# Two reorderings on the matrix engine: earlier transposes in the two output projections, later transposes in the first modulation

## The chip, the cores and the metric

The kernel runs on one core of a Trainium2 chip. The metric is the device time of one execution in microseconds (us), lower is better. A core has a matrix engine (PE in the profile, with PEld for its weight loads), a vector engine (DVE), a scalar engine (ACT), a small general engine (POOL) and a queue engine (SP). Each runs its own list of instructions in order, and they meet through semaphores. Matrix results land in PSUM, everything else lives in SBUF.

## The reference

Two layers of a diffusion backbone over 512 latent and 256 context tokens (six tiles of 128 tokens), model width 1024, everything in float32. Cut to what matters here:

```python
m_lat = split(silu(c)     @ mod_w[l] + mod_b[l], 6)     # shift, scale, gate for mixer and FFN
m_ctx = split(silu(c_ctx) @ mod_w[l] + mod_b[l], 6)
h = modulate(rms(x, norm_pre_mix[l]), m[0], m[1])
o = mixer(h)            # layer 0: gated linear attention (GLA) + softmax attention; layer 1: HGRN2
x = x + m[2] * rms(o @ w_out, norm_post_mix[l])         # output projection, post-norm, gate
h = modulate(rms(x, norm_pre_ffn[l]), m[3], m[4])
x = x + m[5] * rms((silu(h @ w_gate) * (h @ w_up)) @ w_down, norm_post_ffn[l])
```

Layer 0 carries all six tiles, layer 1 ends with the four latent tiles.

## The kernel before

A float32 product is done as three matrix instructions on operands that are split into a high and a low part (`wH`, `wL` for weights: a cast on ACT, then a subtraction on DVE).

**The order.** A scheduler (the tile framework) places instructions on the engines from the order in which the program issues them and from its own costs. Where `self.pinned` is set, the matrix engine keeps the program's order; the other engines are still arranged by the scheduler. In the even mixer of layer 0 the program's order is a string of step names, each of which advances a generator by one step:

```python
run("qk0 qk0 e m qk0 e e v0 ... m m kv q m m q m q m m m m m m m m m qk1 kv m")
```

Here `q` is a block of 48 matrix instructions of the attention's query projection (`nat<-wH,x`, 128x256 each; its first call only loads weights), `kv` the same for keys and values, `qk1` the second half of the GLA queries and keys, and `m` one step of `mod_vec`.

**The early modulation (`mod_vec`).** It makes m[2] and m[3] of layer 0. For each of the two jobs DVE adds up eight scaled rows of `mod_w` into two accumulators (`macc<-mraw`, L535/L537, one `m` step a row block). Then one `m` step sums them over partitions on PE (`mod_acc`, 8 matrix instructions) and DVE copies the sum out (`modrows`, L469). The next step turns it on PE (`modT`, four transposes), and DVE adds the bias (`modcol`, L481) and multiplies the norm's gain in (`gc`, L644). The step after that turns this too (`gcT`, one transpose), DVE copies it (`gt`, L650) and ACT issues its write to DRAM (`gd<-gt`, L652); the same step then starts the second job. `modrows`, `gt` and, later, the attention's table tile `rope` share one ring of two buffers (tag `mraw`). `mod_acc`, `modT` and `gcT` share a ring of two PSUM buffers (tag `tr`).

**The output projections (`out_proj`, called by `project` once a layer).** Tiles are taken in pairs, six tiles in the order 4, 5, 0, 1, 2, 3 in layer 0, and 0, 1, 2, 3 in layer 1. A tile's product is two halves of 24 matrix instructions (`oproj`, 128x512). The first pair's is cut so that the late weight units come last; the other pairs run tile by tile, half by half. After a tile, `end` runs its post-norm, residual and pre-norm: ACT squares (`junk<-oproj`), DVE multiplies (`pn`), POOL takes the power (`rs`), DVE adds (`xr`), ACT squares again (`xn<-xr`), POOL again, DVE writes the normalized tile (`xn<-xr,rs`, L695). It leaves a *turn* in the list `self.turns`: eight transposes on PE in two PSUM buffers (`hT<-ident,xn`), eight activations on ACT (`f<-hT`, L707), and a split (`b<-f`, L97 on ACT and L98 on DVE) into the operands of the feed-forward block. `turn(left)` runs turns from the front of that list until `left` are left:

```python
def turn(self, left=0):
    while len(self.turns) > left:
        self.turns.pop(0)()
```

The third tile of a layer's projection (and the fifth in layer 0) is the point at which two turns, of the two tiles before it, are waiting. The last pair's turns run in the feed-forward block's first products (`pearly`).

Of the kernel before, what the change touches and what calls it, by code (L numbers as in the profile page):

```python
# [316 lines left out]
class Net:  # L317
# [761 lines left out]
    def even_mixer(self, h, mix, z):  # L1079
# [132 lines left out]
        def run(steps):  # L1212
            for x in steps.split():
                if x not in running:
                    running[x] = kinds[x]()
                next(running[x], None)

        self.pinned = True
        run("qk0 qk0 e m qk0 e e v0 qk0 e e m qk0 e e m v0 e e m m q v0 m m v0 m m kv q m m q m q m m m m m m m m m qk1 kv m")
        tp.release()  # L1220
        gp = self.open_pool("gla")
        run("c0 l0 kv m c0 kv c0 v1 qk1 c0 p p qk1 c0 l0 p qk1 l0 c0 g0 qk1 l0 p c1 p v1 l0 p v1 l0 c1 p v1 l0 c1 l1 g1 g0 c1 g0 r0 c1 l1 r0 g0 l1")
# [335 lines left out]
    def out_proj(self, wop, pp, w, cat, tiles, end, mods=iter(())):  # L1558
        self.tc.keep_in_program_order(self.nc.scalar.preload_act_table_set("silu_and_others"))
        units = [self.rows_unit(w, c) if c < 4 else self.rows_unit(w, c, wop) for c in range(KD)]  # L1560
        for t0 in range(0, len(tiles), 2):
            pair = tiles[t0 : t0 + 2]
            pts = [self.mm_tile("oproj") for _ in pair]
            for cs in ((0, 1, 2, 3), (4, 5, 6, 7)) if t0 == 0 else (range(KD),):
                for t, pt in zip(pair, pts):
                    tok = slice(t * P, (t + 1) * P)
                    for hf in range(2):
                        n = slice(hf * 512, hf * 512 + 512)
                        for c in cs:
                            self.mm3(  # L1570
                                pt[:, n],
                                cat.hl(c, tok),
                                (units[c][0][:, 0, n], units[c][1][:, 0, n]),
                                c == 0,
                                c == KD - 1,
                            )
                        if hf or t0:
                            next(mods, None)
                    if cs[0] == 0 and t == pair[len(cs) == 4]:
                        self.turn()  # L1580
            for t, pt in zip(pair, pts):
                for _ in end(pt, t):
                    pass
# [622 lines left out]
```

## Time and profile before

| | |
|---|---|
| median of 3 runs | 1681.66 us (1681.48 to 1682.79) |
| the profiled execution's own time | 1680.08 us |
| its span | 1678.3 us |
| PE busy | 1638.8 us, 98% |
| DVE busy | 1312.2 us, 78% |
| ACT busy | 916.9 us, 55% |
| granted PE clock | 0.999 |
| early modulation's turns | 102 to 118 us |
| layer 0's projection | 340 to 417 us |
| layer 1's projection | 1285 to 1334 us |

The profile is one execution; all times in it count from the start of its span. "Busy" is time in which an engine has an instruction under way. In a timeline, each row is a start, a length, an engine, a line, an operation with output and inputs, and a count; in brackets stands how long the engine was idle before it and what it waited for. Matrix instructions overlap, so the distance between starts is their price, not their length.

### The profile page before, as it was taken

How to read it: one execution, taken by the hardware profiler on the slowest of the kernel's cores; microseconds unless marked ns; L12 is line 12 of the kernel's file. 1: busy time of each engine (PE TensorE's matmuls, PEld its weight loads, DVE VectorE, ACT ScalarE, POOL GpSimd, SP SyncE). 2: the span in 40 equal slices, each digit the busy share in tenths (PEclk: the TensorE clock that was granted, in tenths of full speed). 3: DMA queues.
4: the chain of work that ended last, by engine and by line, in shares of the span. 5: the costliest groups of instructions: out<-in, count | busy, mean ns of one | idle time of the engine just before them, and what ended most of it. 6: DMA issues, size and time to landing. Idle time of an engine off the chain costs nothing.

```text
span 1678.3 us, 32400 instructions
## 1 busy us (share of the span) xinstructions
PE 1638.8 (98%) x13347; PEld 1474.3 (88%) x13347; DVE 1312.2 (78%) x2104; ACT 916.9 (55%) x1560; POOL 122.6 (7%) x129
## 2 busy tenths in 40 slices
PE   6999998999999999999999999999999999999998
PEld 5889987888999999998887788888888899999886
DVE  4889768966898989778668648788775499987887
ACT  4745557846544443445447536566564565555564
POOL 1004210001000000002101000000000100000310
PEclk9999999999999999999999999999999999999999
DMA  9651002154253446249516542111115334433973
GB/s 331 193 155 41 2 28 101 52 198 152 90 151 101 134 148 193 78 136 222 101 56 210 193 132 64 52 54 50 52 56 159 117 113 122 115 101 101 223 166 138
DMA packets 184736, 204.77 MB, mean 122 GB/s; under 512 B 7143, under 2 KB 141837, under 8 KB 184589
## 3 DMA queue, kind: packets, MB, share of 16 engines
q1 hardware_dynamic: 173632, 181.82, 34.6%
q0 software_dynamic: 9024, 17.30, 5.9%
q10 hardware_dynamic: 1932, 3.59, 0.6%
q8 instruction: 104, 1.70, 0.4%
q14 instruction: 44, 0.35, 0.1%
HBM read 193.23 MB, written 9.46 MB: 121 GB/s over the span
## 4 chain that ended last, share of the span: by engine, by line
PE 84%; DVE 7%; ACT 4%; DMA 2%; issue 2%; POOL 1%; DVEq 0%; ACTq 0%; POOLq 0%
PE nat L355 12%; PE a L355 11%; PE ff L355 8%; PE E L355 8%; PE x L355 6%; PE oproj L355 6%; PE o L355 4%; PE b L355 4%; PE D L355 4%; PE pearly L355 3%; PE fq L355 3%; PE gqk L355 2%; PE q L355 2%; PE S L355 2%; PE poh L355 1%
## 5 line engine op out<-in xcount | busy, mean ns | idle before, releaser
L355 PE MATMUL nat<-wH,x 128*128 128x256 f32 (+2 forms) x968 | 226.1, 322 | 3.1 <-ACT x L734 2.6
L355 PEld LDWEIGHTS nat<-wH,x 128*128 128x128 f32 x968 | 162.0, 190 | 20.5 <-ACT x L734 4.2
L824 ACT CAST wH<-raw 128x1024 fp32r<-128x1024 f32 x120 | 124.9, 1051 | 99.0 <-DVE raw L849 37.6
L825 DVE TENSOR_TENSOR wL<-raw,wH 128x1024 fp32r<-128x1024 f32 x120 | 145.7, 1221 | 23.2 <-ACT wH L824 22.6
L355 PE MATMUL nat<-wL,x 128*128 128x256 f32 (+2 forms) x484 | 153.5, 317 | 1.8 <-DVE wL L770 1.8
L770 DVE TENSOR_TENSOR wL<-raw,wH 128x1024 fp32r<-128x1024 f32 (+1 forms) x83 | 98.7, 1198 | 49.7 <-ACT wH L769 49.0
L355 PE MATMUL ff<-x,wH 128*128 128x512 f32 (+1 forms) x512 | 127.7, 340 | 0.0
L769 ACT CAST wH<-raw 128x1024 fp32r<-128x1024 f32 (+1 forms) x83 | 84.9, 1035 | 70.6 <-PE ff L355 19.9
L668 POOL TENSOR_TENSOR rs<-ms,neghalf 128x1 f32<-128x1 f32 (+2 forms) x62 | 64.7, 1049 | 791.1 <-DVE ms L666 791.0
L355 PE MATMUL oproj<-wH,x 128*128 128x512 f32 x320 | 102.3, 396 | 0.6 <-ACT x L1290 0.6
L355 PEld LDWEIGHTS nat<-wL,x 128*128 128x128 f32 x484 | 92.1, 190 | 7.9 <-DVE wL L770 2.7
L355 PEld LDWEIGHTS ff<-x,wH 128*128 128x128 f32 x512 | 87.2, 190 | 10.0
L597 DVE SCALAR_TENSOR_TENSOR macc<-mraw,scT,macc 128x1024 f32<-128x1024 f32 x70 | 88.0, 1280 | 8.8 <-DMA mraw<-in_mod_w_dram 8.4
L355 PE MATMUL x<-wH,two 128*128 128x512 f32 x280 | 90.6, 392 | 0.8 <-DVE y L1801 0.7
L976 ACT COPY qkh<-arr 128x512 f32<-128x512 f32 x112 | 70.1, 642 | 36.4 <-DVE arr L981 32.2
L1723 POOL DMA_DIRECT2D t<-in_ffn_w_down_dram x36 | 41.8, 1198 | 637.2 <-DVE t L1762 337.5
L355 PE MATMUL ff<-x,wL 128*128 128x256 f32 (+1 forms) x256 | 86.2, 337 | 0.0
L849 DVE TENSOR_TENSOR raw<-raw 128x512 f32<-128x512 f32 x120 | 82.8, 690 | 2.8
L981 DVE TENSOR_TENSOR arr<-arr,f 128x512 f32<-128x512 f32 x112 | 74.2, 687 | 1.9 <-ACT qkh L976 0.3
L355 PEld LDWEIGHTS oproj<-wH,x 128*128 128x128 f32 x320 | 59.5, 188 | 12.8 <-ACT x L1290 1.1
L355 PE MATMUL E<-x,wH 128*128 128x384 f32 (+1 forms) x320 | 70.7, 310 | 0.0
L355 PE MATMUL b<-x,wH 128*128 128x384 f32 (+1 forms) x320 | 70.6, 310 | 0.0
(420 smaller groups left out, 4530.2 us busy)
## 6 DMA issues: line engine op xcount, KB each, us to landing
mraw<-in_mod_w_dram SPq DMA_DIRECT2D x80, 512.0 KB, 4.1
raw<-in_ffn_w_gate_dram SPq DMA_DIRECT2D x44, 512.0 KB, 4.8
raw<-in_ffn_w_up_dram SPq DMA_DIRECT2D x44, 512.0 KB, 4.4
raw<-in_odd_w_in_dram SPq DMA_DIRECT2D x40, 512.0 KB, 3.7
t<-in_ffn_w_down_dram POOLq DMA_DIRECT2D x30, 512.0 KB, 8.7
raw<-in_ffn_w_down_dram SPq DMA_DIRECT2D x28, 512.0 KB, 7.9
mraw<-in_mod_w_dram SPq DMA_DIRECT2D x32, 256.0 KB, 6.3
raw<-in_even_w_in_dram SPq DMA_DIRECT2D x16, 512.0 KB, 6.8
```

Of the source, the lines that this page charges most:

```text
L355: return self.pin(self.nc.tensor.matmul(*a, **k))
L597: nc.vector.scalar_tensor_tensor(a, u, w, a, op0=ALU.mult, op1=ALU.add)
L668: nc.gpsimd.tensor_tensor(rs, ms, self.neghalf.to_broadcast([P, w]), op=ALU.pow)
L769: nc.scalar.copy(H[:, :m], raw[:, :m])
L770: nc.vector.tensor_tensor(L[:, :m], raw[:, :m], H[:, :m].bitcast(F32), op=ALU.subtract)
L824: self.nc.scalar.copy(H, f)
L825: self.nc.vector.tensor_tensor(L, f, H.bitcast(F32), op=ALU.subtract)
L849: add = lambda o, x, y: nc.vector.tensor_tensor(o, x, y, op=ALU.add)
L976: nc.scalar.copy(qkv[:, :, :, half, :], dst)
L981: nc.vector.tensor_tensor(dst, dst, tb, op=ALU.mult)
L1723: add = lambda o, src: self.pin(nc.gpsimd.dma_start(out=o, in_=src, accum_op=ALU.add))
```

## The change

Two edits, no instruction added or removed.

```diff
@@ even_mixer
-        run("... m m kv q m m q m q m m m m m m m m m qk1 kv m")
+        run("... m m kv q m q m q m m m m m m m m m m qk1 kv m")
@@ out_proj, after each half (hf) of each tile
+                        if not hf and t0 and t == pair[0]:
+                            self.turn(1)
                         if hf or t0:
                             next(mods, None)
                     if cs[0] == 0 and t == pair[len(cs) == 4]:
                         self.turn()
```

The first edit puts each of the two steps after `mod_acc` one `q` block later: `modT` behind a block, and `gcT` behind the next, right ahead of the second job's `mod_acc`. The second edit runs the first of the two waiting turns after the first half of the third (and fifth) tile; the other one stays after the second half.

On PE, around the early modulation, before (`nat` is a `q` block, of which only the edges are shown, `macc_795` and `macc_796` the first job's accumulators):

```order
L355 MATMUL nat<-wL,x_356 128x256
L355 MATMUL nat<-wH,x_357 128x256
L355 MATMUL mod_acc<-macc_795,one 32x512 x2
L355 MATMUL mod_acc<-macc_796,one 32x512 x2
L358 MATMUL modT<-ident,modrows 128x128 x4
L355 MATMUL nat<-wH,x_354 128x256
```

and in the changed kernel, the same place, and then the end of the third `q` block (`macc_1341` and `macc_1342` are the second job's accumulators):

```order
L355 MATMUL nat<-wL,x_356 128x256
L355 MATMUL nat<-wH,x_357 128x256
L355 MATMUL mod_acc<-macc_795,one 32x512 x2
L355 MATMUL mod_acc<-macc_796,one 32x512 x2
L355 MATMUL nat<-wH,x_354 128x256
L355 MATMUL nat<-wL,x_354 128x256
```

```order
L355 MATMUL nat<-wL,x_356 128x256
L355 MATMUL nat<-wH,x_357 128x256
L358 MATMUL gcT_1334<-ident,gc_1282 16x128
L355 MATMUL mod_acc<-macc_1341,one 32x512 x2
L355 MATMUL mod_acc<-macc_1342,one 32x512 x2
L355 MATMUL nat<-wH,x_354 128x256
```

The four `modT` transposes now stand one block behind the `mod_acc` that feeds them. DVE, which the scheduler rearranges, has this between the two copies `modrows` before:

```order
L537 SCALAR_TENSOR_TENSOR macc_1291<-mraw_1359,scT,macc_1291 128x1024
L481 TENSOR_TENSOR modcol_794<-modT,col 128x8 x2
L537 SCALAR_TENSOR_TENSOR macc_1292<-mraw_1359,scT,macc_1292 128x1024
L644 TENSOR_TENSOR gc_1232<-modcol_794,col 128x16
L537 SCALAR_TENSOR_TENSOR macc_1291<-mraw_1363,scT,macc_1291 128x1024
L537 SCALAR_TENSOR_TENSOR macc_1292<-mraw_1363,scT,macc_1292 128x1024
L537 SCALAR_TENSOR_TENSOR macc_1291<-mraw_1367,scT,macc_1291 128x1024
L537 SCALAR_TENSOR_TENSOR macc_1292<-mraw_1367,scT,macc_1292 128x1024
L650 COPY gt_1286<-gcT_1284 16x128
L770 TENSOR_TENSOR wL<-raw,wH 128x1024
```

and this in the changed kernel:

```order
L537 SCALAR_TENSOR_TENSOR macc_1341<-mraw_1359,scT,macc_1341 128x1024
L537 SCALAR_TENSOR_TENSOR macc_1342<-mraw_1359,scT,macc_1342 128x1024
L537 SCALAR_TENSOR_TENSOR macc_1341<-mraw_1363,scT,macc_1341 128x1024
L537 SCALAR_TENSOR_TENSOR macc_1342<-mraw_1363,scT,macc_1342 128x1024
L481 TENSOR_TENSOR modcol_794<-modT,col 128x8 x2
L537 SCALAR_TENSOR_TENSOR macc_1341<-mraw_1367,scT,macc_1341 128x1024
L644 TENSOR_TENSOR gc_1282<-modcol_794,col 128x16
L537 SCALAR_TENSOR_TENSOR macc_1342<-mraw_1367,scT,macc_1342 128x1024
L770 TENSOR_TENSOR wL<-raw,wH 128x1024
L650 COPY gt_1336<-gcT_1334 16x128
```

The accumulations of the second job moved ahead of `modcol` and `gc`, and `gt` moved behind the first `wL` of the next weights. ACT's write `gd<-gt` moved with it: before, it stood ahead of the two casts `wH`, now it stands behind them and ahead of the GLA's copies `arrg<-gqk`; the load `rope<-in_const_rope` moved from ahead of the copies `qkg<-arrg` that follow those to behind the first five of them.

On PE, at layer 1's third tile, the difference (`xn_14077` is the first tile's, `xn_14098` the second's) is that the first tile's eight transposes come 24 matrix instructions earlier,

```order
 L355 MATMUL oproj<-wL,x_13845 128x512
 L355 MATMUL oproj<-wH,x_13846 128x512
+L358 MATMUL hT_14132<-ident,xn_14077 128x128 x4
+L358 MATMUL hT_14143<-ident,xn_14077 128x128 x4
 L355 MATMUL oproj<-wH,x_13843 128x512
 L355 MATMUL oproj<-wL,x_13843 128x512
```

and that the second tile's, which were placed in two groups of four amid the fourth tile's product, take the place that the first tile's had:

```order
 L355 MATMUL oproj<-wL,x_13845 128x512
 L355 MATMUL oproj<-wH,x_13846 128x512
-L358 MATMUL hT_14156<-ident,xn_14077 128x128 x4
-L358 MATMUL hT_14167<-ident,xn_14077 128x128 x4
+L358 MATMUL hT_14176<-ident,xn_14098 128x128 x4
+L358 MATMUL hT_14187<-ident,xn_14098 128x128 x4
 L355 MATMUL oproj<-wH,x_13843 128x512
 L355 MATMUL oproj<-wL,x_13843 128x512
```

In layer 0's first such place the first turn comes 20 matrix instructions earlier than before and the second one, whole, 3 later than the first one was; at the second such place (the fifth tile) four groups of four become one group of eight, ahead of the fifth tile's second half, and two groups of four behind it.

More of the change, by code (lines that the diff above doesn't have):

```diff
@@ L1218, in even_mixer @@
         self.pinned = True
-        run("qk0 qk0 e m qk0 e e v0 qk0 e e m qk0 e e m v0 e e m m q v0 m m v0 m m kv q m m q m q m m m m m m m m m qk1 kv m")
+        run("qk0 qk0 e m qk0 e e v0 qk0 e e m qk0 e e m v0 e e m m q v0 m m v0 m m kv q m q m q m m m m m m m m m m qk1 kv m")
         tp.release()
```

## The prediction

> **What bounds the kernel now.** The page comes first: its span, its first engine row and its chain of work.
>
> ```profile
> span 1678.3 us, 32400 instructions
> PE 1638.8 (98%) x13347; PEld 1474.3 (88%) x13347; DVE 1312.2 (78%) x2104; ACT 916.9 (55%) x1560; POOL 122.6 (7%) x129
> PE 84%; DVE 7%; ACT 4%; DMA 2%; issue 2%; POOL 1%; DVEq 0%; ACTq 0%; POOLq 0%
> ```
>
> PE is busy 98% of the span and carries 84% of the chain that ended last. No edit takes instructions away, so time can only be won where PE stands still or is broken up: 1678.3 - 1638.8 = 39.5 us over the whole program, far less at the places of the change. Which waits these are is read from the list of PE's waits between 100 and 200 us, which has one row, and from the timelines of PE, DVE and ACT there.
>
> ```profile
> PE modT L358 <- DVE modrows L469: 1.7, 1, 1.7
> 102.08 1.06 PE L355 MATMUL mod_acc<-macc,one 128*32 128x512 f32 x8
> 104.81 0.66 PE L358 MATMUL modT<-ident,modrows 128*128 128x128 f32 x4 [1.66 <-DVE modrows L469]
> 105.22 0.36 PE L355 MATMUL nat<-wH,x 128*128 128x256 f32 x1
> 111.05 0.27 PE L358 MATMUL gcT<-ident,gc 128*16 128x128 f32 x1
> 117.00 1.06 PE L355 MATMUL mod_acc<-macc,one 128*32 128x512 f32 x8
> 104.07 0.68 DVE L469 COPY modrows<-mod_acc 128x512 f32<-128x512 f32 x1
> 107.29 4.87 DVE L537 SCALAR_TENSOR_TENSOR macc<-mraw,scT,macc 128x1024 f32<-128x1024 f32 x4
> 112.37 0.32 ACTq L652 DMA_DIRECT2D gd<-gt  x1
> 115.67 1.05 ACT L769 CAST wH<-raw 128x1024 fp32r<-128x1024 f32 x1 [3.83 <-PE nat L355]
> 147.45 0.37 ACT L1028 COPY kng<-knpg 128x256 f32<-128x256 f32 x1
> 148.03 1.09 PE L355 MATMUL pdg<-gvo,kng 128*64 128x128 f32 x16
> ```
>
> To be seen: PE issues `modT` right behind the `mod_acc` that it turns, and stands 1.66 us until DVE has copied that sum out (104.07 + 0.68 = 104.75). That is the only listed PE wait in these 100 us. The chance of any larger effect hangs on how closely the other engines follow PE behind it.
>
> **Edit one, the early modulation.** *Removed:* the 1.66 us wait. A `q` block lasts 111.05 - 105.22 = 5.8 us, and `modrows` needs until 104.75, 1.7 us into it. *Cover behind it:* the block now ends near 103.1 + 5.8 = 108.9, then `modT`. On DVE four accumulations now stand ahead of `modcol`; at 4.87 / 4 = 1.22 us each from 104.75 they end at 109.6, so `modcol` and `gc` are done before 112, and `gcT`, a whole block behind `modT`, comes at about 115.1. The second job's sums end near 112.2 (now 107.29 + 4.87 = 112.16) and its `mod_acc` comes near 115.2 instead of 117.00, with 3 us in hand. If that cover were gone, PE would wait for the sums one for one. *What follows PE:* the ACT cast at 115.67 was released by PE's `nat`, so the next weights, and with them DVE's line into the GLA, also come 1.7 us earlier. *What is late next:* the tightest consumer that I find is `pdg` at 148.03, whose `kng` ends at 147.45 + 0.37 = 147.82, 0.21 us before. The write `gd<-gt`, whose issue of 0.32 us stood at 112.37 in idle ACT time, now stands in front of the GLA's copies and can cost 0.1 us beyond that slack. I take -1.6 us. The ends: -1.66 if all of it passes; -0.2 if the rearranged DVE and ACT lines come no earlier at all, as then `pdg` gives back all but its slack.
>
> **Edit two, the price of a turn on PE.** Layer 1's third tile shows both ways in which transposes can stand in a product.
>
> ```profile
> 1320.61 0.39 PE L355 MATMUL oproj<-wL,x 128*128 128x512 f32 x1
> 1320.84 0.39 PE L355 MATMUL oproj<-wH,x 128*128 128x512 f32 x1
> 1321.07 1.03 PE L358 MATMUL hT<-ident,xn 128*128 128x128 f32 x8
> 1321.86 0.48 PE L355 MATMUL oproj<-wH,x 128*128 128x512 f32 x1
> ...
> 1323.55 0.39 PE L355 MATMUL oproj<-wL,x 128*128 128x512 f32 x1
> 1323.89 0.66 PE L358 MATMUL hT<-ident,xn 128*128 128x128 f32 x4
> 1324.30 0.70 PE L355 MATMUL oproj<-wH,x 128*128 128x512 f32 x2
> ...
> 1325.54 0.40 PE L355 MATMUL oproj<-wL,x 128*128 128x512 f32 x1
> 1325.81 0.66 PE L358 MATMUL hT<-ident,xn 128*128 128x128 f32 x4
> 1326.22 0.47 PE L355 MATMUL oproj<-wH,x 128*128 128x512 f32 x1
> ```
>
> The pitch of the product is 1320.84 - 1320.61 = 0.23 us. A group of eight costs 1321.86 - 1320.84 - 0.23 = 0.79; the two groups of four, which had to wait for ACT to empty a PSUM buffer, cost 0.75 - 0.23 = 0.52 and 0.68 - 0.23 = 0.45. Two groups of eight without a wait therefore save 0.97 - 0.79, about 0.2 us a place. At layer 0's first place this holds too; at its second one four groups become three, with `mod_acc` still among them, and I take 0, between -0.2 and +0.2, one such difference either way.
>
> *Are the sources there?* Layer 0's first place, with one row of layer 1 at the end:
>
> ```profile
> 372.41 0.75 DVE L695 TENSOR_SCALAR xn<-xr,rs 128x1024 f32<-128x1024 f32 x1
> 373.13 1.28 DVE L597 SCALAR_TENSOR_TENSOR macc<-mraw,scT,macc 128x1024 f32<-128x1024 f32 x1
> 373.30 1.52 POOL L668 TENSOR_TENSOR rs<-ms,neghalf 128x1 f32<-128x1 f32 x1 [1.29 <-DVE ms L666]
> 378.77 1.04 PE L358 MATMUL hT<-ident,xn 128*128 128x128 f32 x8
> 380.23 0.75 DVE L695 TENSOR_SCALAR xn<-xr,rs 128x1024 f32<-128x1024 f32 x1 [0.44 <-POOL rs L668]
> 1317.35 0.75 DVE L695 TENSOR_SCALAR xn<-xr,rs 128x1024 f32<-128x1024 f32 x1 [0.66 <-POOL rs L668]
> ```
>
> The first turn comes 20 x 0.23 = 4.6 us earlier, near 374.2; its `xn` ends at 372.41 + 0.75 = 373.16, 1.0 us ahead. The second turn comes 3 x 0.23 + 0.79 = 1.5 us behind the old 378.77, near 380.25, while its `xn` ended at 380.23 + 0.75 = 380.98: PE would wait 0.73 us, and the rest of the product behind it in PE's list waits too. But that `xn` waited for POOL's `rs`. The POOL row quoted takes 1.52 us and ends at 374.82, 0.41 us behind DVE's accumulation beside it (374.41). In the changed list DVE has the shorter `b<-f` (128x512 against the accumulation's 128x1024 in 1.28 us, so I estimate 0.64) beside that `rs`, so `xn` comes about 0.6 earlier and the wait is some 0.14. The page "SBUF — State Buffer" of the Trainium skill, section "SBUF: two separate sides", says that a DVE instruction with two SBUF inputs and a reading POOL instruction exclude each other for a whole instruction; by that the wait is 0.14 and the whole sum below -2.7, without it 0.73 and -2.1, and the row (1.52 us, ending behind DVE) agrees with the rule. I take -0.2 + 0.14, about -0.1; the ends are -0.2 and 0.73 - 0.2 = +0.5. In layer 1 the second source ends at 1318.10, 3 us before its turn: no wait.
>
> *What the earlier turn does to ACT.* Layer 1, from the third tile's end on:
>
> ```profile
> 1324.50 1.28 DVE L755 SCALAR_TENSOR_TENSOR xr<-pn,rs,xr 128x1024 f32<-128x1024 f32 x1 [0.73 <-POOL rs L668]
> 1328.86 1.15 ACT L676 ACTIVATE xn<-xr 128x1024 f32<-128x1024 f32 x1
> 1329.90 3.04 ACT L769 CAST wH<-raw 128x1024 fp32r<-128x1024 f32 x3
> 1331.68 3.49 DVE L770 TENSOR_TENSOR wL<-raw,wH 128x1024 fp32r<-128x1024 f32 x3
> 1344.87 0.66 PE L358 MATMUL hT<-ident,xn 128*128 128x128 f32 x4 [0.73 <-ACT f L707]
> 1349.78 0.39 PE L355 MATMUL pearly<-x,wH 128*128 128x256 f32 x1 [1.15 <-DVE x L98]
> ```
>
> The third tile's `xr` was ready at 1325.78, but ACT squared it only at 1328.86, behind both turns' sixteen activations. Half of these now run earlier. The tile itself ends 0.8 us later, as eight transposes now stand ahead of its end, so its `xr` comes near 1326.6 and the square some 1328.86 - 1326.6 = 2.3 us earlier than it did. DVE began `wL` (no idle before it) at 1331.68, though the first cast was done by 1329.90 + 1.01 = 1330.9. With DVE free by then, `wL` ends 0.8 to 1.1 us earlier, since the casts themselves wait for PE to free their buffers and end at 1332.94, with one `wL` of 1.16 us behind. Behind `wL`, in DVE's order, stand the puts and the fourth tile's post-norm, and behind those its turn, which carries PE's two waits, 0.73 and 1.15 us. So I take 0.8 us of these 1.88, and with the 0.2 of the groups -1.0 us; the ends are -0.2 (the chain is held elsewhere) and -0.2 - 1.88 = -2.1.
>
> **Sum.** -1.6 - 0.1 + 0 - 1.0 = -2.7 us. The profiled execution took 1680.08 us, 1.8 around its span; it becomes 1677.4. The median of the runs shown, 1681.66, is 1.6 above it, and goes to 1679.0. All good ends together: -1.66 - 0.2 - 0.2 - 2.1 = -4.2, 1677.5. All bad ends: -0.2 + 0.5 + 0.2 - 0.2 = +0.3, 1682.0.
>
> **Rivals.** Changes under 0.2% (3.4 us) are about what a measurement of this kernel cannot tell from none.
>
> *All of it passes (0.30).* Layer 1's two waits vanish whole, as the chain behind them is long enough to be shifted by 2 us, and the rest comes at its good end: 1677.5. For it: PE is the chain. Against: the casts' release by PE holds `wL` to about 1 us.
>
> *Only the seams move (0.12).* The kernel does what it says, but `pdg` and its like take back the first edit's gain, and layer 1's chain is held by the load of the fourth weight unit: -0.2 - 0.1 - 0.2, 1681.2. Against: the releasing rows on ACT and DVE are PE's own.
>
> *A DMA issue stops ACT: slower (0.13).* `gt` now is written when `wL` is, and `gd<-gt` is issued near 117. The table tile `rope` shares its ring, so the load of `rope` must wait until that write has landed, and ACT, which issues it, stops with the GLA's copies queued behind it and `pdg` behind those.
>
> ```profile
> 122.83 1.01 ACT L976 COPY qkg<-arrg 128x256 f32<-128x256 f32 x2
> DMA to landing us min/median/max: 2.0/2.0/2.0
> DMA to landing us min/median/max: 4.2/8.2/12.1
> ```
>
> The load's new place is behind that copy (123.84, less one 512-column copy and the 1.7 us: near 121.6). The trace doesn't show when the old write landed. The nearest row is the output's writes, the 2.0 us; the slowest that I found are loads of `ffn_w_down`, the last row, up to 12.1. At 2.0 it lands by 119, with no stall. At 12.1 ACT stops 117 + 12.1 - 121.6 = 7.5 us, PE loses 7.3 of it behind the slack of 0.2, and 7.3 - 2.7 = +4.6 gives 1686.3. The sign turns at a landing of 7.6 us. The row of writes is nearer in kind, hence the small chance.
>
> **The numbers.** My forecast has 0.45, within 0.2%. Faster by over 0.2%: 0.30. Within: 0.45 + 0.12 = 0.57. Slower: 0.13. The range 1677.0 to 1682.3 leaves out the stall and little else: it takes in both ends of the sum, 1677.5 and 1682.0, with a few tenths for the spread of runs.
>
> **What would show it.** Right: no wait at `modT` and the second job's `mod_acc` near 115.3; `hT` in groups of eight at all but one place, with a PE wait under 0.2 us at layer 0's second turn; ACT's square of layer 1's third tile some 2 us sooner after that tile's product; PE's waits at 1344.87 and 1349.78 down by 0.8 us together. Wrong: ACT idle ahead of `rope<-in_const_rope`; a new PE wait at `pdg`; a wait of 0.7 us at layer 0's second turn; or the two waits in `pearly` as long as before.

## The result and the profile after

| | before | after |
|---|---|---|
| median of 15 runs each | 1681.97 us (1680.64 to 1682.79) | 1679.01 us (1677.85 to 1681.13) |
| ratio, 95% interval | | 0.9985 (0.9979 to 0.9992) |
| the profiled execution | 1680.08 us | 1681.13 us |

By the medians the changed kernel is 2.96 us faster. (The ratio in this and the later tables is not the quotient of the two medians, which here is 0.9982.) Its profiled execution was the longest of its 15, and that of before is shorter than all 15 runs of before; so the two profiles lie 1.05 us apart in the wrong order, and a whole span says nothing here. What can be read is how far PE is ahead or behind at one and the same instruction, place by place.

The page's first lines (span, then busy time of each engine) show that no work was taken away:

```profile
span 1679.4 us, 32397 instructions
PE 1639.6 (98%) x13347; PEld 1474.1 (88%) x13347; DVE 1313.1 (78%) x2104; ACT 917.3 (55%) x1560; POOL 122.5 (7%) x129
```

**The early modulation.** The list of PE's waits between 100 and 200 us (one row again, but another), then PE's, ACT's and DVE's timelines there:

```profile
PE pcg L355 <- issue: 0.2, 1, 0.2
101.74 1.06 PE L355 MATMUL mod_acc<-macc,one 128*32 128x512 f32 x8
108.59 0.60 PE L358 MATMUL modT<-ident,modrows 128*128 128x128 f32 x4
114.79 0.27 PE L358 MATMUL gcT<-ident,gc 128*16 128x128 f32 x1
114.99 1.06 PE L355 MATMUL mod_acc<-macc,one 128*32 128x512 f32 x8
116.07 0.32 ACTq L652 DMA_DIRECT2D gd<-gt  x1
119.33 1.00 ACT L976 COPY qkg<-arrg 128x512 f32<-128x512 f32 x2 [0.20 <-DVE arrg L1268]
119.93 0.35 ACTq L1300 DMA_DIRECT2D rope<-in_const_rope_dram  x1
120.23 1.02 ACT L976 COPY qkg<-arrg 128x256 f32<-128x256 f32 x2
145.48 0.37 ACT L1028 COPY kng<-knpg 128x256 f32<-128x256 f32 x1
146.03 1.09 PE L355 MATMUL pdg<-gvo,kng 128*64 128x128 f32 x16
161.35 0.38 PE L355 MATMUL pcg<-qkg 64*32 64x32 f32 x20 [0.16 <-issue]
167.60 1.91 PE L355 MATMUL pbg<-qkg 64*64 64x64 f32 x64
```

`modT` has no wait. From one `mod_acc` to the next PE needs 114.99 - 101.74 = 13.25 us, where before it was 117.00 - 102.08 = 14.92: 1.67 us less, the wait of 1.66 whole. ACT does not stand still ahead of the `rope` load. `pdg` has 146.03 - 145.85 = 0.18 us behind `kng`, so it takes nothing back at this place. What is new is a pause inside a run of `pcg` matmuls, whose releaser the trace does not name ("issue").

**Layer 0's projection.** PE, DVE and POOL at the second turn; the first row is of the profile of before, the `rs` for which the second turn's `xn` waited there:

```profile
378.67 1.52 POOL L668 TENSOR_TENSOR rs<-ms,neghalf 128x1 f32<-128x1 f32 x1 [3.85 <-DVE ms L666]
372.58 1.04 PE L358 MATMUL hT<-ident,xn 128*128 128x128 f32 x8
376.86 0.68 DVE L98 TENSOR_TENSOR b<-f,b 128x512 fp32r<-128x512 f32 x1
377.02 0.93 POOL L668 TENSOR_TENSOR rs<-ms,neghalf 128x1 f32<-128x1 f32 x1 [3.86 <-DVE ms L666]
377.99 0.76 DVE L695 TENSOR_SCALAR xn<-xr,rs 128x1024 f32<-128x1024 f32 x1 [0.44 <-POOL rs L668]
378.89 1.06 PE L358 MATMUL hT<-ident,xn 128*128 128x128 f32 x8
```

Both turns are groups of eight. `rs` took 0.93 us where it took 1.52, `xn` ended at 378.75, and PE's `hT` behind it has no listed wait. It starts 0.44 us behind the product instruction ahead of it, though, where the pitch is 0.23, so about 0.2 us was lost there.

**Layer 1's projection.** PE's first `oproj`, the turns, ACT's square of the third tile, the last turn in `pearly`, the wait behind it, and PE's first product behind the projection. The *put* is the subtraction `x<-f,x` (L98) in which DVE writes the low half of the last tile's operand; `f<-f` (L121) is a difference of operand blocks for later products. The first fence has places of the profile of before that are not shown yet:

```profile
1284.57 0.53 PE L355 MATMUL oproj<-wH,x 128*128 128x512 f32 x1 [0.39 <-ACT x L1290]
1321.33 1.02 ACT L676 ACTIVATE junk<-oproj 128x1024 bf16<-128x1024 f32 x1 [4.83 <-PE oproj L355]
1343.54 0.60 PE L358 MATMUL hT<-ident,xn 128*128 128x128 f32 x4
1345.28 0.36 PE L355 MATMUL pearly<-x,wH 128*128 128x256 f32 x1
1361.35 0.40 PE L355 MATMUL a<-b,wH 128*128 128x256 f32 x2
```

```profile
1285.34 0.50 PE L355 MATMUL oproj<-wH,x 128*128 128x512 f32 x1 [0.39 <-ACT x L1290]
1316.57 1.03 PE L358 MATMUL hT<-ident,xn 128*128 128x128 f32 x8
1322.91 1.04 PE L358 MATMUL hT<-ident,xn 128*128 128x128 f32 x8
1323.11 1.02 ACT L676 ACTIVATE junk<-oproj 128x1024 bf16<-128x1024 f32 x1 [2.36 <-PE oproj L355]
1327.59 1.06 ACT L676 ACTIVATE xn<-xr 128x1024 f32<-128x1024 f32 x1
1344.20 1.24 PE L358 MATMUL hT<-ident,xn 128*128 128x128 f32 x8
1345.19 0.49 PE L355 MATMUL pearly<-x,wH 128*128 128x256 f32 x2
1347.82 1.22 DVE L121 TENSOR_TENSOR f<-f 128x1024 f32<-128x1024 f32 x1
1348.95 0.69 DVE L98 TENSOR_TENSOR x<-f,x 128x512 fp32r<-128x512 f32 x1
1349.69 0.39 PE L355 MATMUL pearly<-x,wH 128*128 128x256 f32 x1 [1.14 <-DVE x L98]
1361.26 0.40 PE L355 MATMUL a<-b,wH 128*128 128x256 f32 x2
```

This stretch took 1361.35 - 1284.57 = 76.78 us and takes 1361.26 - 1285.34 = 75.92 now: 0.86 less. The wait of 0.73 at the last turn is no longer listed: from its first transpose to the next product PE needs 0.99 us, where it needed 1.74. A group of eight without a wait costs 0.79, so about 0.2 us is left. The wait of 1.15 behind it is 1.14.

**What one profile hides.** The table gives the same differences for every profile taken: how much longer (+) or shorter (-) than in the profile of before PE needs for a stretch, in us. The stretches: from `mod_acc` to `mod_acc` (102 to 117); the GLA from `pog` at 156 to `pbg` at 167; from layer 0's first `oproj` to its first `pearly`; layer 1 as above; the rest of layer 1's gate and up products, from that `a` to the `o` products at 1578, in which the profile of before is the shortest of all thirteen.

| profile | modulation | GLA | layer 0 | layer 1 | FFN, layer 1 |
|---|---|---|---|---|---|
| after, first | -1.67 | +0.38 | -0.08 | -0.86 | +1.10 |
| after, second | -1.68 | +0.97 | -0.08 | -0.77 | +0.58 |
| after, third | -1.68 | +0.66 | -0.10 | -1.40 | +0.79 |
| edit one alone | -1.68 | +0.38 | +0.01 | +0.12 | +0.44 |
| edit two alone | +0.15 | 0.00 | -0.07 | -0.87 | +0.48 |
| edit two, layer 1 | -0.02 | +0.01 | +0.01 | -0.81 | +0.63 |
| edit two, layer 0 | -0.02 | 0.00 | -0.11 | +0.33 | +0.68 |
| turns spaced later | +0.08 | +0.02 | -0.02 | -0.91 | +0.03 |
| gate's turn close | +0.17 | +0.81 | -0.09 | -1.06 | +0.24 |
| put before sum | -1.68 | +0.61 | -0.14 | -2.17 | +0.92 |
| puts chained | -1.68 | +0.38 | -0.09 | -1.99 | +0.59 |
| puts chained, again | -1.68 | +0.66 | -0.12 | -1.88 | +0.88 |

The front of layer 1's stretch, which the second edit does not touch, alone differs by -0.19 to +0.31 between the profiles. From the third tile's first product on, the six profiles that have the second edit there as it is read -0.87 to -1.33, the two that lack it -0.09 and +0.01. Of this the projection's product has -0.27 to -0.29, the price of the groups. The rest, -0.59 to -1.06, is nearly all at the last turn: from its first transpose to the next product 1.74 us before and 0.79 to 1.18 now.

### The profile page after: what moved, and what is told of

Its sections match the earlier page's. It is cut to its first block, busy times and chain, and to the rows that moved or that the text cites. A ratio compares the mean times of both kernels' runs of the same rounds, so it can differ in the third digit from the quotient of the medians.

```text
span 1679.4 us, 32397 instructions
## 1 busy us (share of the span) xinstructions
PE 1639.6 (98%) x13347; PEld 1474.1 (88%) x13347; DVE 1313.1 (78%) x2104; ACT 917.3 (55%) x1560; POOL 122.5 (7%) x129
## 4 chain that ended last, share of the span: by engine, by line
PE 80%; DVE 9%; DMA 4%; ACT 4%; issue 2%; POOL 1%; SPq 0%; DVEq 0%; ACTq 0%; POOLq 0%
PE nat L355 12%; PE a L355 10%; PE ff L355 8%; PE E L355 7%; PE oproj L355 6%; PE x L355 5%; PE o L355 4%; PE b L355 3%; PE D L355 3%; PE fq L355 3%; PE gqk L355 2%; PE pearly L355 2%; PE q L355 2%; PE S L355 2%; PE poh L355 1%
## 5 line engine op out<-in xcount | busy, mean ns | idle before, releaser
L355 PE MATMUL E<-T,wH 128*128 128x384 f32 (+1 forms) x320 | 70.4, 309 | 0.3 <-DVE go L902 0.3
```

The costliest lines, as they stand in the source:

```text
L355: return self.pin(self.nc.tensor.matmul(*a, **k))
```

## Experiments

Each median is of 11 runs, beside runs of the kernel before on the same chip: 33 in the first two groups, 27 in the third.

### The parts of the change, and the whole again

Edit one alone is the new order string without the new turn, edit two alone the new turn with the old string. For layer 1 alone:

```diff
-                        if not hf and t0 and t == pair[0]:
+                        if not hf and t0 and t == pair[0] and len(tiles) == 4:
                             self.turn(1)
```

Edit one alone: 

> Edit one alone: the new order of the early modulation, no turn moved. Theory (what PE gains in front of the GLA passes to the end): no wait at the first modT, the seams give back 0.0 to 0.4 us, so the median is 1.3 to 1.7 us under that of the kernel before. Rival (only the seams move): pdg and the writes behind it take the 1.66 us back, median 0.2 us under. The first edit's share of the measured 3.0 us is what this run leaves to it.

Edit two alone: 

> Edit two alone: the half tile's turn in the product of layer 0 and of layer 1, the early modulation as before. Theory: -0.1 us in layer 0 and -1.0 us in layer 1, and both pass to the end: median 1.1 us under the kernel before. Rival (the profile of the changed kernel lost 1.07 us again in layer 1's first products of the FFN, between 1376 and 1428 us): given back there as a rule, the median is 0.0 to 0.2 us under.

Layer 1 alone: 

> Edit two in layer 1 alone. Theory: -1.0 us at the projection and its first pearly group, which passes: median 1.0 us under the kernel before, so within 0.2 us of edit two in both layers. Rival: given back in the FFN behind it: median 0.0 to 0.2 us under, and the profile's PE is 1 us ahead at 1345 and level with before at 1430.

The whole: 

> The changed kernel once more, for a second profiled execution and a median on the same chip as its parts. Theory: the parts add up: edit one alone plus edit two alone equal the whole, 2.7 to 3.0 us under the kernel before; and the 2.3 us that its first profile lost at the start of layer 0's down product, and the 1.07 us after 1376 us, are that one execution's and are not there again. Rival: they are there again, as DVE's and the weight loads' pace sets these stretches.

| kernel | median, us | against before (1681.36) | ratio, 95% interval |
|---|---|---|---|
| edit one alone | 1680.02 | -1.34 | 0.9992 (0.9983 to 1.0001) |
| edit two alone | 1679.69 | -1.67 | 0.9990 (0.9982 to 0.9999) |
| edit two, layer 1 | 1679.87 | -1.49 | 0.9992 (0.9983 to 1.0000) |
| the whole | 1678.68 | -2.68 | 0.9980 (0.9971 to 0.9989) |

The parts add up: 1.34 + 1.67 = 3.01 against 2.68 and, in the first measurement, 2.96. The whole reaches the end. That each edit does so by itself is less sure: an interval is 0.0017 of the time wide, 2.9 us, and edit one's includes no change. So the split is read with the table: the modulation's 1.68 stands in every profile that has the first edit whole, layer 1's 0.8 to 1.4 in every one that has the second as it is, and neither in one whose order there is that of before. In its own profile edit one gives 0.38 back in the GLA, which leaves 1.68 - 0.38 = 1.30; the 1.34 of the time is near to it, but could not have told it from 0.5.

The changed kernel's first profile also lost some 2 us at the start of layer 0's down product. PE's waits between 740 and 810 us, first in that profile, then with edit one alone:

```profile
PE x L355 <- DVE wL L1759: 0.5, 1, 0.5
PE o L355 <- DVE two L1760: 0.4, 1, 0.4
PE x L355 <- DVE two L1760: 0.3, 1, 0.3
```

```profile
PE o L355 <- DVE two L1758: 0.9, 1, 0.9
```

In the other eleven profiles the list is empty there, those of the changed kernel's second and third execution too. So it comes and goes with the execution. Both profiles that have it are among the eight with a changed order string, which is too few to tie it to the string or to clear the string of it.

The loss in layer 1's products is smaller but came again, +0.58, and edit one alone, which changes nothing in layer 1's projection, has +0.44. In the profile of layer 1 alone PE is 0.84 us ahead of before at that `a` and 0.26 ahead from 1428 us on, close to the sign that the rival had named. The rival that edit two's gain is given back there is not borne out by the times (1.67 and 1.49 under before, where it had 0.0 to 0.2), though a part may be: with edit two as it is the loss is 0.24 to 1.10, in the three profiles without it 0, 0.44 and 0.68. These overlap; how much belongs to the edit stays open.

### Layer 0 alone

The same condition with `len(tiles) == 6`. 

> Edit two in layer 0 alone, modulation and layer 1 as before. Theory (prediction's term): PE at the end of layer 0's projection 0.1 us ahead, the second turn without a listed wait because rs on POOL is stretched by a shorter DVE instruction (0.93 us in the changed kernel, 1.52 before); median within 0.3 us of before. Rival (edit two's 1.67 against 1.49 us for layer 1 alone understates it): 0.5 us or more under before.

Measured: 1680.95 us against 1681.01, ratio 1.0004 (0.9995 to 1.0013); in the profile -0.11 at the projection, and no listed wait at the second turn. The prediction's term stands, and the time can tell no such difference.

### Edit one without its cover

```diff
-        run("... kv q m q m q m m m m m m m m m m qk1 kv m")
+        run("... kv q m q m m q m m m m m m m m m qk1 kv m")
```

> The changed kernel, but gcT stands right behind the moved modT instead of a block later: the cover of edit one's second step is taken away and the block count is the same. DVE's gc ended at 110.75 us in the changed kernel's first profile and modT at 109.19. Theory (without the block as cover PE waits for DVE's line one for one): a new wait of 1.5 to 1.6 us at gcT, all of edit one's gain is lost, and the median is that of edit two alone, 1.4 to 1.6 us above the changed kernel; and as PE is no earlier in the GLA, the pause of 0.2 to 0.5 us at pcg (161 to 162 us), seen in all three profiles with edit one and in none of the three without it, is not there. Rival: DVE or the cast of the next weights is the bound there, and PE gets the wait back before 163 us: within 0.5 us of the changed kernel.

Measured: 1680.61 us against 1680.85, ratio 0.9997 (0.9988 to 1.0006). PE's and DVE's timelines:

```profile
108.51 0.60 PE L358 MATMUL modT<-ident,modrows 128*128 128x128 f32 x4
110.49 0.17 DVE L644 TENSOR_TENSOR gc<-modcol,col 128x16 f32<-128x16 f32 x1
110.80 0.27 PE L358 MATMUL gcT<-ident,gc 128*16 128x128 f32 x1 [1.70 <-DVE gc L644]
116.75 1.06 PE L355 MATMUL mod_acc<-macc,one 128*32 128x512 f32 x8
161.91 1.19 PE L355 MATMUL pcg<-qkg 64*32 64x32 f32 x108
163.54 0.38 PE L355 MATMUL pcg<-qkg 64*32 64x32 f32 x20 [0.45 <-issue]
```

The wait is back at the next consumer, 1.70 us, and the modulation's column reads +0.17 instead of -1.67: without a block between the turn and its next use the edit is worth nothing at this place. The second half of the expectation is wrong. PE is no earlier here than before, and yet it pauses at the same `pcg` matmul. The pause stands in all eight profiles with a changed order string and in none of the five with the old one, so it goes with the order, not with PE's lead. It and the few tenths around it cost 0.38 to 0.97 us. The wait puts this kernel level with edit two alone, and the pause 0.81 us behind that; by the runs' distance to before it is 1.67 - 0.24 = 1.43 behind, two distances from different chips with such wide intervals. What PE waits for there is taken up in the last section.

### The turns spaced, but later

```diff
@@ out_proj
+                        if not hf and t0 and t == pair[1] and len(tiles) == 4:
+                            self.turn()
                         if hf or t0:
                             next(mods, None)
                     if cs[0] == 0 and t == pair[len(cs) == 4]:
-                        self.turn()
+                        self.turn(1 if t0 and len(tiles) == 4 else 0)
```

> Layer 1 alone, with the early modulation and layer 0 as before: the two turns are spaced as in edit two, but later instead of earlier: the first where both stood, the second half a tile behind it, in the fourth tile's product. Both get groups of eight. Theory (the gain comes from activations that leave ACT's queue ahead of the third tile's square; the groups are worth 0.1 to 0.2): eight activations still stand ahead of that square as in edit two, so the wait of 0.73 us goes here too, and the median is 0.8 us under before. Rival (it is the earlier place that counts, since the second turn's activations now arrive at 1327 us and push the square and the casts of the weights back): only the groups' 0.1 to 0.2 us is won, and PE's wait at the last hT stays at 0.7 us or more.

Measured: 1680.17 us against 1680.85, ratio 0.9996 (0.9987 to 1.0005). ACT's and PE's timelines:

```profile
1326.25 1.06 ACT L676 ACTIVATE xn<-xr 128x1024 f32<-128x1024 f32 x1
1328.49 1.85 ACT L707 ACTIVATE f<-hT,modcol,aff 128x128 f32<-128x128 f32 x5 [1.09 <-PE hT L358]
1331.76 2.98 ACT L769 CAST wH<-raw 128x1024 fp32r<-128x1024 f32 x3
1341.08 0.39 PE L355 MATMUL pearly<-b,wL 128*128 128x256 f32 x1 [1.29 <-DVE wL L770]
1345.26 1.04 PE L358 MATMUL hT<-ident,xn 128*128 128x128 f32 x8
```

Both theories saw half. The third tile's square is 2.6 us sooner than before (1326.25 against 1328.86), since only eight activations stand ahead of it, and both waits of before, 0.73 and 1.15, are gone from the list. But the second turn's activations now stand ahead of the weight casts (1331.76 against 1329.90), and PE waits 1.29 for a `wL` made from them. The second wait went only because PE, held up there, comes later to its place: the difference `f<-f` still stands ahead of the put on DVE. In sum -0.91, much as edit two: 0.73 + 1.15 - 1.29 = 0.59 and the groups. In this one profile, then, it is the spacing that pays, and the place decides which wait is paid; the time agrees (-0.68), but its interval includes no change.

### The wait that did not move

The changed kernel, in layer 1: `f<-f` (line 121) queued behind the first half's put, and in the second kernel the next difference behind the second half's put as well, and the first weight cast of the products behind the first sum's cast. `after(b, a)` queues `b` behind `a` on their engine; the code is cut to these lines of the second kernel (the first one has the first two), and the rest of the edit collects the instructions that they name.

```diff
+        first = v.tensor_tensor(b11, b11, b12, op=ALU.subtract)
...
+            self.net.after(first, puts[0][1])
...
+            self.net.after(second, puts[1][1])
+            self.net.held = t1
```

First kernel: 

> The changed kernel, with the last tile's first half put into its operand on DVE ahead of the difference f<-f that stands before it now (1347.82, 1.22 us, in the first profile of the changed kernel), in layer 1 alone; the order of the instructions behind it follows as the scheduler sees it. PE's last wait of 1.14 us at the pearly products was the same in all six profiles, whatever the turns did. Theory: it is that one DVE instruction's 1.22 us, so it goes, and the median is 0.8 to 1.1 us under the changed kernel. Rival: the second half's put, behind the next difference, is late next, and PE waits some 0.5 to 1 us there; then the median is within 0.4 us of the changed kernel.

Second kernel: 

> As the run before, and besides the second half's put stands ahead of DVE's second difference, and the first weight cast of the next products behind the first sum's cast. Theory: both puts come in time, no wait in pearly, 0.9 to 1.2 us under the changed kernel. Rival: DVE, 93 to 97% busy from 1360 us on, gets the sums and weights later by what it idles ahead of the second put (up to 1 us), and PE waits that long in the first products of the FFN: within 0.3 us of the changed kernel.

The second again, 

> The kernel with both puts of layer 1 ahead of the differences, beside the changed kernel on the same chip. Theory (DVE's idle before the second put is paid back in the first products of the FFN): within 0.4 us of the changed kernel. Rival (a real gain that the spread of the first comparison hid): 0.9 us or more under it.

with the changed kernel beside it: 

> The changed kernel on the same chip as the next run, for a direct comparison. Theory: 2.3 to 3.0 us under before; in the profile a pause at pcg (0.16 or 0.45 us), as in every profile so far with the moved modulation turns.

| kernel | median, us | before | ratio, 95% interval |
|---|---|---|---|
| put before sum | 1678.68 | 1680.85 | 0.9983 (0.9974 to 0.9992) |
| puts chained | 1678.50 | 1680.85 | 0.9983 (0.9974 to 0.9991) |
| puts chained, again | 1679.00 | 1681.01 | 0.9991 (0.9982 to 1.0000) |
| changed kernel beside it | 1678.45 | 1681.01 | 0.9985 (0.9976 to 0.9994) |

DVE's timeline in the chained kernel, and PE's row at the place:

```profile
1342.59 1.38 PE L365 MATMUL hT<-ident,xn 128*128 128x128 f32 x8
1346.35 0.69 DVE L98 TENSOR_TENSOR x<-f,x 128x512 fp32r<-128x512 f32 x1
1346.95 1.22 DVE L123 TENSOR_TENSOR f<-f 128x1024 f32<-128x1024 f32 x1
1348.69 0.68 DVE L98 TENSOR_TENSOR x<-f,x 128x512 fp32r<-128x512 f32 x1
```

The put now stands ahead of the difference, PE has no wait in `pearly`, and layer 1's column, -0.77 to -1.40 in the changed kernel's three profiles, goes to between -1.88 and -2.17. So the wait of 1.14 was one DVE instruction of 1.22 us in front of the put. The time doesn't follow: on one chip the chained kernel is 0.55 us above the changed one. The next column reads +0.59 to +0.92, but the changed kernel's own three read +0.58 to +1.10, so nothing more is given back there. Of these two kernels on that chip the profiles, too, differ little: -1.88 against -1.40 at the place, and spans of 1676.5 and 1676.6 us. It is a gain at its place, 0.5 us there and 1.0 by the means of three profiles each, that no run showed at the end; neither kernel beats the changed one.

## Why the prediction was right, step by step

*The total.* -2.7 was predicted, 1679.0; the runs gave 1679.01, and -2.96, -2.68 and -2.56 against before on three occasions. That 1679.0 was met to 0.01 us is luck: the start it was counted from, 1681.66, was 0.31 below the median of all 15 runs, and the change 0.3 too small. The parts agree less closely than the total.

*Edit one, -1.6.* The wait, its cover and the place of the second `mod_acc` (predicted 115.2, found 114.99) came as worked out, 1.67 us. What failed is the step on what follows: the prediction looked for the tightest semaphore, found 0.21 us at `pdg`, and allowed 0.1 for it. `pdg` held. The loss, 0.38 to 0.97, came 15 us later, around an instruction that waits for nothing named. The term was worth 0.7 to 1.3 us in the profiles: within its ends, but too large as taken. The time, 1.34, lies as near to it as its interval can say.

*Layer 0, -0.1 and 0.* Found -0.07 to -0.14 together. The POOL row that the prediction quotes (373.30) is the one for which this tile's `xr` waited, a step before its `xn`; the one ahead of `xn` (378.67) took 1.52 us as well and ended 0.41 us behind DVE's accumulation too, so the working stands. The second turn rested on POOL's `rs` being held up by DVE's instruction beside it; `b<-f` was estimated at 0.64 and took 0.68, `rs` ended at 377.95, 0.41 behind it as before, and `xn` came so late only that about 0.2 us was lost, where 0.14 was worked out. The section "SBUF: two separate sides" of the page "SBUF — State Buffer" of the Trainium skill gives the rule used, and these rows agree with it; a third case is in the profile of before, where a DVE instruction of two operands, one of them PSUM's `oproj`, left `rs` at 0.56 us, where with no DVE instruction beside it (388.90 us) it takes 0.55:

```profile
371.28 1.22 DVE L746 TENSOR_TENSOR pn<-oproj,gv 128x1024 f32<-128x1024 f32 x1
371.44 0.56 POOL L668 TENSOR_TENSOR rs<-ms,neghalf 128x1 f32<-128x1 f32 x1 [3.86 <-DVE ms L666]
```

*Layer 1, -1.0.* Found -0.77 to -1.40 in the six profiles with this edit, on average -0.96. The mechanism held: the third tile's square came 1327.59 - 1323.11 = 4.48 us behind that tile's `junk`, which the end of its product releases, and before it was 1328.86 - 1321.33 = 7.53: 3.05 us sooner, where the working has 3.1 (2.3, and the 0.8 by which that end comes later). The groups gave 0.27 to 0.29 for the 0.2 worked out, the chain 0.59 to 1.06 for the 0.8. The working was wrong in one step: it took 0.8 us out of "PE's two waits, 0.73 and 1.15", as if one chain carried both. It carries the first only, of which nothing is left in two of the six profiles and 0.2 to 0.4 us in the other four (the last turn takes 0.79 us in those two and 0.99 to 1.18 in these). The second comes from a DVE instruction in front of a put and was there in all six, 1.05 to 1.14 us. The good end of -2.1, and with it the rival in which all passes, was therefore out of reach by 1.15. Where nothing is left the turn gained 1.74 - 0.79 = 0.95, some 0.2 more than the listed wait, as its two groups of four are one of eight there; the working had not counted this.

*The rivals.* Only the seams move: its -0.5 lies outside the interval of the result, which at 0.9979 to 0.9992 is -3.5 to -1.3 us. All of it passes: its 1677.5, -4.2, lies outside on the other side, and would have needed that second wait. A DMA issue stops ACT: the `rope` load was issued at 119.93 and the copy behind it began at 120.23 with no idle time ahead of either, so the write of `gt`, issued at 116.07, cost nothing. (The landing time at which that rival changes its sign is 7.5 us by its own terms, 117 + 7.5 - 121.6 - 0.2 = 2.7, not 7.6.)

## What to carry to other kernels

A wait of the busiest engine for something just handed to another can be won whole at its place by putting one block of its own work between the two, if every later use has such a block too: here the 1.67 us came back as 1.70 with the gate's turn left close. How much of it reaches the end is another question: 0.4 to 1.0 us was lost again 45 us later. Two waits in a row on one engine need not have one cause; before they are added, look at what stands just ahead of the releasing instruction on its own engine. And where single executions differ by 1 us, compare the same stretch in several profiles rather than the ends of two.

## What was not expected of the hardware

PE paused for 0.16 to 0.45 us at the 109th of 128 `pcg` matmuls whenever the order string was changed, even where PE was no earlier, with no semaphore to account for it; with the old string the same 128 ran without a break:

```profile
162.04 1.35 PE L355 MATMUL pcg<-qkg 64*32 64x32 f32 x128
```

The trace holds a candidate, which no run tested: the fetch of PE's own instructions. The page of the changed kernel has this row (queue, kind: packets, MB, share of the DMA engines):

```profile
q8 instruction: 104, 1.70, 0.4%
```

All its packets have 16,384 bytes, which is 64 bytes for each of PE's 26,694 matmuls and weight loads, so this is probably PE's queue (an estimate). In all eight profiles with the pause such a packet starts 232 of these instructions ahead of the 109th matmul, and PE goes on 2.45 to 2.78 us after the packet's start. In the five without it the packet starts 253 to 261 instructions, and 3.1 to 3.6 us, ahead of the same matmul. The pause also follows the packet's length: 0.16 to 0.17 us in the four profiles in which the packet took at most 1.17 us, 0.43 to 0.45 in the four in which it took at least 1.22. The only other PE pauses of this kind behind the first 20 us, 0.30 to 0.33 us at `pch` in layer 1 in three profiles, come 2.2 to 2.5 us after such a packet's start. All this fits a run of small matmuls that uses up its instructions before the next packet is in, and an order string that shifts where in the run that happens. As no run changed the fetch alone, the cause stays argued, not shown.
